# GpSimd's 1024-column subtractions in a one-core transformer layer, issued as two of 512 columns

## The chip, the core and the metric

The kernel runs on one core of a Trainium2 chip. Five engines work side by side, each through its own queue and in order: TensorE (PE in the profile; its weight loads are PEld), VectorE (DVE), ScalarE (ACT), GpSimd (POOL) and SyncE (SP), which here issues nearly all DMAs. They meet through semaphores. The metric is the time on the device in microseconds.

## The reference

One layer of a hybrid transformer: sequence 2048, width 1024, float32. After an RMS norm, a projection to 2576 columns is split over three mixers: differential attention (4 heads with two 64-wide query and key maps each, a bias by distance, causal), a gated linear attention in chunks of 64, and a pooling over windows of 2, 4, 8 and 16 positions. Their outputs are joined, projected and added to the input. Then comes a gated feed-forward part with 2816 hidden columns.

```python
hn = rms_norm(h, attn_norm_g[l])
proj = jnp.einsum('bsd,de->bse', hn, w_in[l])
...
a_out = diff_attention(q, k, v, lam, bias_by_dist)
...
mixed = jnp.concatenate([a_out, b_out, c_out], axis=-1)
h = h + jnp.einsum('bse,ed->bsd', mixed, w_out[l])
hn = rms_norm(h, ffn_norm_g[l])
ff = jax.nn.silu(jnp.einsum('bsd,df->bsf', hn, w_gate[l])) * jnp.einsum('bsd,df->bsf', hn, w_up[l])
h = h + jnp.einsum('bsf,fd->bsd', ff, w_down[l])
```

## The kernel before

**Number format.** Each large product is made of three: an operand x is kept as a high part H, which is x in TensorE's float32r format, and a low part L = x - H in the same format. A product of two such operands is H·H + H·L + L·H. So every weight tile that is loaded has to be split: ScalarE casts it (H), and another engine subtracts (L).

**Stages.** The tokens are handled in four blocks of 512. Phase 1, up to about 620 us, makes the projections of all blocks; its weights are split by ScalarE and VectorE in pieces of 512 columns. Beside it run the gated linear attention and the attention of the first block. Phase 2 makes, block by block, the output projection (L1312 to L1314, eight column tiles), gate and up products (the same lines, or L1384) and the down products (L133, added up by VectorE at L1349), while the attention of blocks 1 to 3 runs beside blocks 0 and 1 until about 1815 us. Blocks 2 and 3 use a scheme with seven instead of eight half-size products (`unit`, L1384), for which sums of weight quarters are formed first (L512 to L515) and sums of activations in `tprep` (L1247 to L1266).

**Weights in phase 2.** `pump` issues the DMA of the next raw weight (L572) when a raw buffer is free, and starts a preparation when one of the ring's weight buffers is free. `wprep` splits a raw weight of 1024 columns: L543 is ScalarE's cast, L544 GpSimd's subtraction, and L548 stores the result for use by later blocks. For blocks 2 and 3 `wpair` fetches the stored split of two quarters and splits the sums of quarters with its helper `hl`: L494 is the cast, L495 the subtraction. A weight buffer holds H in columns 0 to 1023 and L in columns 1024 to 2047. TensorE reads it in row tiles of 128 columns; the low part is the operand of L1314 and of the third product in the down and unit products.

**Attention.** Per unit of 256 queries: scores on TensorE (L133 with the tiles at<-qd and kd, banks 64 to 68), their move out of PSUM by VectorE (L943, with the bias L947), exponentials by ScalarE (L955), the combination of the two maps by VectorE (L963, three operands in SBUF), transposes (L988), and the values product.

**Order.** The Python program spawns generators for these chains and advances them at each `tick`. The order in which an engine gets its instructions is then written by the framework's scheduler (`schedule_with_timeline_sim=True`), which works from its own durations of the instructions. So an instruction of another size can change the order of others, too.

Of the kernel before, what the change touches and what calls it, by code (L numbers as in the profile page):

```python
# [13 lines left out]
ALU = mybir.AluOpType  # L14
# [18 lines left out]
def f(ap):  # L33
    return ap.bitcast(F32)


def r3(ap, a):
    return ap.rearrange("p (a b) -> p a b", a=a)
# [49 lines left out]
def body(nc, tc, V, G, ACT, PE, DMA, A, banks, dram):  # L88
# [354 lines left out]
    def kept(k, i):  # L443

        if (k, i) not in keep:
            keep[k, i] = dram(f"wk{k}{i}", [P, 2048])
        return keep[k, i]
# [35 lines left out]
    def wpair(p):  # L483

        key = pieces[p][0]
        r0, r1 = raws.pop(p)[:, :1024], raws.pop(p + 1)[:, :1024]
        d = W2[key] = {}

        def put(op, w, o):
            d[op] = (r3(w[:, o:o + 512], 4), r3(w[:, 1024 + o:1536 + o], 4), w)  # L490
            uses2[id(w)] = uses2.get(id(w), 0) + 1

        def hl(w, src, o=0, n=1024):
            ACT.copy(w[:, o:o + n], src)  # L494
            G.tensor_tensor(w[:, 1024 + o:1024 + o + n], src, f(w[:, o:o + n]), op=ALU.subtract)  # L495
        k, g = key[0].lower(), key[2]
        w = yield from wring.acq()
        DMA.dma_start(f(w[:, :2048]), kept(k, GS * g))
        put("A11", w, 0)
        put("A12", w, 512)  # L500
        if wst["half"] is None:
            w = yield from wring.acq()
            wst["half"], o = w, 0
            uses2[id(w)] = 1
        else:
            w, o = wst["half"], 512
            wst["half"] = None
            uses2[id(w)] -= 1
        DMA.dma_start(f(r3(w[:, :2048], 2)[:, :, o:o + 512]), r3(kept(k, GS * g + 1), 2)[:, :, 512:1024])
        put("A22", w, o)  # L510
        a11, a12, a21, a22 = r0[:, :512], r0[:, 512:], r1[:, :512], r1[:, 512:]
        V.tensor_tensor(a22, a21, a22, op=ALU.add)  # L512
        V.tensor_tensor(a21, a11, a21, op=ALU.subtract)
        V.tensor_tensor(a11, a22, a11, op=ALU.subtract)
        V.tensor_tensor(a12, a12, a11, op=ALU.subtract)  # L515
        w = yield from wring.acq()
        hl(w, r0)
        put("S2", w, 0)
        put("S4", w, 512)
        w = yield from wring.acq()  # L520
        wst["busy"] = False
        hl(w, r1)
        put("S3", w, 0)
        put("S1", w, 512)
        rawring.rel(wst.pop(("raw", p)), wst.pop(("raw", p + 1)))
# [12 lines left out]
    def wprep(p, w):  # L538
        half, k, src, n = pieces[p]
        raw = raws.pop(p)  # L540
        if n == 0:
            wH, wL = w[:, 0:1024], w[:, 1024:2048]
            ACT.copy(wH, raw[:, :1024])  # L543
            G.tensor_tensor(wL, raw[:, :1024], f(wH), op=ALU.subtract)  # L544
            W2[half] = (r3(wH, KT), r3(wL, KT), w)
            rawring.rel(raw)
            if k is not None:
                DMA.dma_start(k, f(w[:, :2048]))  # L548
            return
        a = KT if n == P else 4  # L550
        wH = r3(w[:, 0:a * n], a)
        wL = r3(w[:, 1088:1088 + a * n], a)
        rv = r3(raw[:, :a * n], a)
        wtile.setdefault((half, k), []).append((wH, wL, w))
        h = a // 2
        ACT.copy(wH[:, :h], rv[:, :h])  # L556
        V.tensor_tensor(wL[:, :h], rv[:, :h], f(wH[:, :h]), op=ALU.subtract)  # L557
        ACT.copy(wH[:, h:], rv[:, h:])
        V.tensor_tensor(wL[:, h:], rv[:, h:], f(wH[:, h:]), op=ALU.subtract)
        rawring.rel(raw)  # L560

    def pump():

        while wst["dma"] < len(pieces) and (rawring.free or pieces[wst["dma"]][3] == -2):
            p = wst["dma"]
            half, k, src, n = pieces[p]
            wst["dma"] += 1
            if n == -2:
                continue
            raw = rawring.free.pop(0)  # L570
            m = KT * P if n in (-1, 0, P) else 4 * n
            DMA.dma_start(raw[:, :m], src.rearrange("p a n -> p (a n)") if len(src.shape) == 3 else src)  # L572
            raws[p] = raw
        if wring.free and wst["prep"] < wst["dma"] and not wst["busy"]:
            p = wst["prep"]
            half, k, src, n = pieces[p]
            if n == -1:
                if p + 1 < wst["dma"]:
                    wst["prep"] += 2
                    wst["busy"] = True  # L580
                    wst["raw", p], wst["raw", p + 1] = raws[p], raws[p + 1]
                    spawn(wpair(p))
            elif n == -2:
                wst["prep"] += 1
                w = wring.free.pop(0)
                DMA.dma_start(f(w[:, :2048]), k)
                W2[half] = (r3(w[:, 0:1024], KT), r3(w[:, 1024:2048], KT), w)
            else:
                wst["prep"] += 1
                spawn(wprep(p, wring.free.pop(0)))  # L590
# [498 lines left out]
    for si, (half, k, b) in enumerate(seq):  # L1089
# [11 lines left out]
        if kind == "e":  # L1101
            bank = force(dense.acq())
            wH, wL, _ = wt[0]
# [12 lines left out]
        else:  # L1116
            n = 272 if i == 2 else 256
# [513 lines left out]
```

## Time and profile before

| | us |
|---|---|
| median of 3 runs | 2679.62 |
| lowest and highest | 2678.34, 2682.49 |
| the profiled execution | 2674.36 |
| its span | 2672.5 |
| TensorE busy | 2537.2 (95%) |
| VectorE busy | 1939.9 (73%) |
| ScalarE busy | 1192.2 (45%) |
| GpSimd busy | 911.0 (34%) |

The span is the time from the first to the last instruction of the profiled execution. Busy shares are means over stages with different limits, so what a change is worth has to be read from the stage that it touches. The chain of waits follows the work that ended last back to what released it.

### The profile page before, as it was taken

What the parts mean: (1) busy time and instruction counts of PE and PEld (TensorE: products, weight loads), DVE (VectorE), ACT (ScalarE), POOL (GpSimd) and SP (SyncE); (2) the same over time, 40 slices, a digit from 0 to 9 for tenths busy, and PEclk for the clock granted to TensorE, in tenths of its full rate; (3) what the DMA queues carried; (4) which work ended last, traced back from release to release, by engine and by line L of the source; (5) the groups of instructions that cost most, each with busy time, mean ns of one, the idle gap of its engine ahead of it and who ended that gap; (6) DMA issues with size and microseconds to landing.
All of it is one profiled execution on the core that took longest, in us unless ns stands there. A gap on an engine that the chain in (4) does not pass through costs nothing.

```text
span 2672.5 us, 38997 instructions
## 1 busy us (share of the span) xinstructions
PE 2537.2 (95%) x14064; PEld 2170.1 (81%) x14064; DVE 1939.9 (73%) x4002; ACT 1192.2 (45%) x2275; POOL 911.0 (34%) x595
## 2 busy tenths in 40 slices
PE   7999889989899999999999999979799999999999
PEld 5887778868778888877788888857688989899998
DVE  7769886689678886885777777775573778766665
ACT  3555545357554454453544444443242333433332
POOL 4235432356644433321322222201423332423331
PEclk8999999989999999999999999989899999999999
DMA  5333644335755645456767667545467665676664
GB/s 166 119 118 103 182 153 151 115 105 189 276 179 159 184 137 183 147 184 214 261 232 245 219 219 248 201 149 182 162 235 274 246 229 191 235 260 225 250 249 167
DMA packets 185518, 517.52 MB, mean 194 GB/s; under 512 B 19067, under 2 KB 63660, under 8 KB 158700
## 3 DMA queue, kind: packets, MB, share of 16 engines
q1 hardware_dynamic: 185036, 515.00, 57.2%
q8 instruction: 111, 1.82, 0.3%
q14 instruction: 83, 0.68, 0.1%
q10 hardware_dynamic: 288, 0.02, 0.0%
HBM read 386.10 MB, written 128.84 MB: 193 GB/s over the span
## 4 chain that ended last, share of the span: by engine, by line
PE 74%; DVE 14%; issue 4%; DMA 3%; ACT 3%; POOL 2%; SPq 0%; DVEq 0%; POOLq 0%; ACTq 0%
PE bk L133 30%; PE bk L1384 14%; PE bk L1313 7%; PE bk L1314 7%; PE bk L1312 7%; PE bk L1108 2%; PE bk L1109 2%; PE bk L1110 2%; PE bk L988 2%; DVE at L963 1%; DVE c L250 1%; DVE c L249 1%; DMA at<-qd 1%; ACT at L955 1%; DVE at L943 1%
## 5 line engine op out<-in xcount | busy, mean ns | idle before, releaser
L133 PE MATMUL bk<-p,c 128*128 128x512 f32 x1136 | 312.2, 399 | 9.9 <-DVE p L217 3.9
L1312 PE MATMUL bk<-c,c 128*128 128x512 f32 x680 | 272.8, 402 | 3.5 <-DMA c<-wko 3.5
L1313 PE MATMUL bk<-c,c 128*128 128x512 f32 x680 | 272.5, 401 | 0.0
L1314 PE MATMUL bk<-c,c 128*128 128x512 f32 x680 | 270.9, 399 | 0.1
L133 PEld LDWEIGHTS bk<-p,c 128*128 128x128 f32 x1136 | 209.3, 190 | 53.5 <-DVE p L217 4.3
L955 ACT ACTIVATE at<-at,at 128x1024 f32<-128x1024 f32 (+4 forms) x192 | 171.6, 895 | 170.2 <-DVE at L952 170.0
L1384 PE MATMUL bk<-c,c 128*128 128x256 f32 x1824 | 239.6, 283 | 0.3 <-ACT c L1390 0.3
L544 POOL TENSOR_TENSOR c<-c,c 128x1024 fp32r<-128x1024 f32 x61 | 151.3, 2483 | 258.8 <-ACT c L543 231.2
L1384 PEld LDWEIGHTS bk<-c,c 128*128 128x128 f32 x1824 | 230.2, 190 | 4.5 <-ACT c L1390 0.7
L1349 DVE TENSOR_TENSOR p<-p,bk 128x512 f32<-128x512 f32 x308 | 204.4, 679 | 34.0 <-PE bk L133 33.3
L943 DVE TENSOR_SCALAR_CACHE_REDUCE at<-bk 128x512 f32<-128x512 f32 (+3 forms) x304 | 154.3, 519 | 86.4 <-PE bk L133 85.0
L1108 PE MATMUL bk<-c,c 128*128 128x512 f32 x448 | 185.1, 415 | 18.6 <-ACT c L556 9.4
L133 PE MATMUL bk<-c,at 128*128 128x512 f32 (+4 forms) x704 | 183.9, 357 | 18.0 <-DMA at<-qd 7.0
L133 PE MATMUL bk<-c,c 128*128 128x256 f32 (+2 forms) x1272 | 184.2, 297 | 6.3 <-DVE p L393 3.1
L1109 PE MATMUL bk<-c,c 128*128 128x512 f32 x448 | 184.5, 412 | 5.2 <-DVE c L250 5.2
L1110 PE MATMUL bk<-c,c 128*128 128x512 f32 x448 | 183.0, 408 | 1.4 <-DVE c L557 1.4
L133 PEld LDWEIGHTS bk<-c,c 128*128 128x128 f32 x1272 | 168.5, 190 | 14.9 <-DVE p L393 4.5
L133 PEld LDWEIGHTS bk<-c,at 128*128 128x128 f32 x704 | 120.5, 193 | 45.5 <-DVE at L943 17.6
L1312 PEld LDWEIGHTS bk<-c,c 128*128 128x128 f32 x680 | 129.0, 190 | 33.2 <-DMA c<-wko 4.2
L1314 PEld LDWEIGHTS bk<-c,c 128*128 128x128 f32 x680 | 128.8, 189 | 29.3 <-POOL c L544 0.5
L1313 PEld LDWEIGHTS bk<-c,c 128*128 128x128 f32 x680 | 129.1, 190 | 28.8 <-DVE c L1184 0.3
L133 PE MATMUL bk<-at,c 128*128 128x256 f32 (+1 forms) x856 | 141.8, 286 | 1.4 <-DVE at L993 0.7
(373 smaller groups left out, 5858.4 us busy)
## 6 DMA issues: line engine op xcount, KB each, us to landing
c<-wkd SPq DMA_DIRECT2D x33, 1024.0 KB, 6.6
c<-w_u SPq DMA_DIRECT2D x56, 512.0 KB, 5.7
c<-w_g SPq DMA_DIRECT2D x55, 512.0 KB, 5.7
wkg<-c SPq DMA_DIRECT2D x21, 1024.0 KB, 4.9
c<-kd SPq DMA_DIRECT2D x72, 256.0 KB, 5.2
c<-vd SPq DMA_DIRECT2D x72, 256.0 KB, 4.4
c<-wko SPq DMA_DIRECT2D x18, 1024.0 KB, 6.0
p<-w_g SPq DMA_DIRECT2D x33, 512.0 KB, 5.5
```

Of the source, the lines that this page charges most:

```text
L133: PE.matmul(out, l, r, start=start and i == 0, stop=stop and i == n - 1)
L544: G.tensor_tensor(wL, raw[:, :1024], f(wH), op=ALU.subtract)
L943: V.tensor_scalar(p[:, c0:c0 + far], pt[:, :far], 1.0, None, op0=ALU.mult, op1=ALU.max, accum_out=mx[:, nx:nx + 1])
L955: ACT.activation(p[:, c0:c1], p[:, c0:c1], AF.Exp, bias=nmx, accum_out=u.z[:, i, m, k:k + 1])
L1108: PE.matmul(bank, wH[:, kt, :], hH[:, kt, :], start=st, stop=False)
L1109: PE.matmul(bank, wH[:, kt, :], hL[:, kt, :], start=False, stop=False)
L1110: PE.matmul(bank, wL[:, kt, :], hH[:, kt, :], start=False, stop=sp)
L1312: PE.matmul(bank, wH[:, kt, :], H[:, kt, :], start=st, stop=False)
L1313: PE.matmul(bank, wH[:, kt, :], L[:, kt, :], start=False, stop=False)
L1314: PE.matmul(bank, wL[:, kt, :], H[:, kt, :], start=False, stop=sp)
L1349: V.tensor_tensor(h2[b][d], h2[b][d], bank, op=ALU.add)
L1384: PE.matmul(out, l[:, k, :], r[:, k, :], start=start and k == 0 and n == 0, stop=k == 3 and n == 2, skip_group_check=True)
```

## The change

Both subtractions of 1024 columns that split weights in phase 2 are issued as two of 512 columns each. The first writes the low part's columns 0 to 511, the second 512 to 1023. The operands, ScalarE's casts and all other lines are as before. A line number behind L495 is higher by one in the changed kernel, one behind L544 by two.

```diff
--- before.py
+++ after.py
@@ -492,7 +492,8 @@
 
         def hl(w, src, o=0, n=1024):
             ACT.copy(w[:, o:o + n], src)
-            G.tensor_tensor(w[:, 1024 + o:1024 + o + n], src, f(w[:, o:o + n]), op=ALU.subtract)
+            for c in range(0, n, 512):
+                G.tensor_tensor(w[:, 1024 + o + c:1536 + o + c], src[:, c:c + 512], f(w[:, o + c:o + c + 512]), op=ALU.subtract)
         k, g = key[0].lower(), key[2]
         w = yield from wring.acq()
         DMA.dma_start(f(w[:, :2048]), kept(k, GS * g))
@@ -541,7 +542,8 @@
         if n == 0:
             wH, wL = w[:, 0:1024], w[:, 1024:2048]
             ACT.copy(wH, raw[:, :1024])
-            G.tensor_tensor(wL, raw[:, :1024], f(wH), op=ALU.subtract)
+            for c in (0, 512):
+                G.tensor_tensor(wL[:, c:c + 512], raw[:, c:c + 512], f(wH[:, c:c + 512]), op=ALU.subtract)
             W2[half] = (r3(wH, KT), r3(wL, KT), w)
             rawring.rel(raw)
             if k is not None:
```

GpSimd's queue at the preparation of block 2's activations (trace 1904 to 1950 us). c, p and pp are weight buffers and raw buffers, tp the activations; first before, then now:

```order
L495 TENSOR_TENSOR pp_14950<-c_102,pp_14950 128x1024
L1242 TENSOR_TENSOR c_72<-tp_15421,c_72 128x1024
L1242 TENSOR_TENSOR c_75<-tp_15422,c_75 128x1024
L495 TENSOR_TENSOR p_6371<-c_103,p_6371 128x1024
L495 TENSOR_TENSOR pp_14950<-p_6372,pp_14950 128x1024
L495 TENSOR_TENSOR pp_14950<-c_102,pp_14950 128x1024
```

```order
L496 TENSOR_TENSOR pp_15066<-c_102,pp_15066 128x512 x2
L1244 TENSOR_TENSOR c_72<-tp_15540,c_72 128x1024
L1244 TENSOR_TENSOR c_75<-tp_15541,c_75 128x1024
L496 TENSOR_TENSOR p_6373<-c_103,p_6373 128x512 x2
L496 TENSOR_TENSOR pp_15066<-p_6374,pp_15066 128x512 x2
L496 TENSOR_TENSOR pp_15066<-c_102,pp_15066 128x512 x2
```

Every row of L495 is now two rows of L496 with half the columns, one directly behind the other, which the listing joins as x2. The order of this stretch is otherwise the same.

TensorE's queue where the third query block's attention runs beside the output projection of block 1 (the matmuls that the trace of before has at about 1230 us). bk are PSUM banks, c_74 is K, at_7945 and at_7964 are Q, c_80 the unit matrix of the transposes, c_72, c_73, c_100 and c_101 are activations and weights of the output projection. Before:

```order
L133 MATMUL bk_66<-at_7962,c_83 128x256
L133 MATMUL bk_64<-c_74,at_7945 128x512 x2
L133 MATMUL bk_66<-c_74,at_7945 128x256 x2
L133 MATMUL bk_66<-c_74,at_7945 128x512 x2
L1312 MATMUL bk_61<-c_72,c_100 128x512
L1313 MATMUL bk_61<-c_73,c_100 128x512
L1314 MATMUL bk_61<-c_72,c_100 128x512
```

The scores that follow there, 24 rows of bk_61 and 18 of bk_62 later:

```order
L1314 MATMUL bk_62<-c_72,c_101 128x512
L133 MATMUL bk_65<-c_74,at_7945 128x384 x2
L988 MATMUL bk_67<-c_80,at_7947 128x128
L988 MATMUL bk_67<-c_80,at_7946 128x128
L988 MATMUL bk_67<-c_80,at_7947 128x128
L133 MATMUL bk_66<-c_74,at_7945 128x512 x2
L988 MATMUL bk_64<-c_80,at_7947 128x128
```

And now:

```order
L1316 MATMUL bk_62<-c_72,c_100 128x512
L1315 MATMUL bk_63<-c_73,c_101 128x512
L1316 MATMUL bk_63<-c_72,c_101 128x512
L990 MATMUL bk_67<-c_80,at_7965 128x128
L133 MATMUL bk_65<-c_74,at_7964 128x384 x2
L133 MATMUL bk_66<-c_74,at_7964 128x512 x2
L990 MATMUL bk_64<-c_80,at_7965 128x128
L133 MATMUL bk_65<-c_74,at_7964 128x512 x2
L133 MATMUL bk_66<-c_74,at_7964 128x384 x2
L1314 MATMUL bk_61<-c_72,c_100 128x512
L1315 MATMUL bk_61<-c_73,c_100 128x512
```

The score products into bk_65 and bk_66 stand ahead of the block of bk_61, which they followed before; the transposes into bk_67 and bk_64 have moved with them. The first instruction that stands elsewhere on any engine is one that the trace of before has at about 620 us. The stretch in which TensorE's queue changes most is 900 to 1310 us, by up to 66 places; later it is mostly groups of twelve matmuls that change places.

## Rows read from the trace of the kernel before

**Rows 1.** The page: busy time, share and instructions of each engine, and the chain of waits by engine.

```profile
PE 2537.2 (95%) x14064; PEld 2170.1 (81%) x14064; DVE 1939.9 (73%) x4002; ACT 1192.2 (45%) x2275; POOL 911.0 (34%) x595
...
PE 74%; DVE 14%; issue 4%; DMA 3%; ACT 3%; POOL 2%; SPq 0%; DVEq 0%; POOLq 0%; ACTq 0%
```

**Rows 2.** Busy time of each engine by stretch: the stretch in us from the span's start, its length, then per engine busy us (instructions), the granted clock, the DMA share and GB/s.

```profile
600.00:800.00 200.00, 186.74 (x964) 155.98 (x964) 154.29 (x299) 120.89 (x249) 112.82 (x78) 0.97 0.65 213
800.00:1100.00 300.00, 298.43 (x1486) 248.59 (x1485) 237.14 (x585) 146.90 (x271) 119.72 (x67) 1.00 0.53 163
1100.00:1300.00 200.00, 187.66 (x926) 154.51 (x925) 142.99 (x341) 88.83 (x176) 52.08 (x33) 0.97 0.61 200
...
1700.00:2000.00 300.00, 257.18 (x1383) 215.97 (x1382) 195.38 (x406) 117.37 (x203) 70.20 (x38) 0.92 0.54 187
2000.00:2673.00 673.00, 661.94 (x4448) 608.69 (x4446) 455.29 (x699) 235.03 (x366) 209.73 (x87) 1.00 0.64 231
```

**Rows 3.** GpSimd's subtraction at L544: duration in ns (least, median, most), first and last start in us; below, who waited for the line, in us and times.

```profile
L544 POOL TENSOR_TENSOR c<-c,c x61: 2372/2409/2921, 620.9 to 1744.3; 128x1024 fp32r<-128x1024 f32 x61
...
  ACT c L543: 10.6, 3
  PEld bk L1314: 3.5, 3
  PE bk L1314: 2.5, 2
```

**Rows 4.** The timeline of GpSimd and of VectorE near 2408 us: start us, us, engine and line.

```profile
2408.28 2.41 POOL L495 TENSOR_TENSOR pp<-p,pp 128x1024 fp32r<-128x1024 f32 x1
...
2408.29 2.95 DVE L1426 TENSOR_TENSOR c<-pp,c 128x512 f32<-128x512 f32 x1
...
2412.98 0.69 DVE L1426 TENSOR_TENSOR pp<-c,pp 128x512 f32<-128x512 f32 x1
```

**Rows 5.** Durations (ns: least, median, most) of three lines of VectorE. L963 and L1339 read their operands in SBUF, L1349 reads a PSUM bank.

```profile
L963 DVE SCALAR_TENSOR_TENSOR at<-at,at,at x160: 336/744/2951, 327.7 to 1812.2; 128x512 f32<-128x512 f32 x112, 128x128 f32<-128x128 f32 x16, 128x256 f32<-128x256 f32 x16, 128x384 f32<-128x384 f32 x16
...
L1339 DVE TENSOR_TENSOR c<-c,c x43: 670/692/2909, 743.0 to 1828.6; 128x512 f32<-128x512 f32 x43
...
L1349 DVE TENSOR_TENSOR p<-p,bk x308: 654/678/690, 761.6 to 2668.4; 128x512 f32<-128x512 f32 x154
```

**Rows 6.** The timeline near 1274 us: two instructions of GpSimd and one of VectorE.

```profile
1273.68 2.41 POOL L544 TENSOR_TENSOR c<-c,c 128x1024 fp32r<-128x1024 f32 x1 [1.57 <-ACT c L543]
1276.05 1.76 POOL L1203 TENSOR_TENSOR p<-p,c 128x512 f32<-128x512 f32 x1
...
1274.85 1.79 DVE L1302 SCALAR_TENSOR_TENSOR c<-p,c,c 128x512 fp32r<-128x512 f32 x1 [0.50 <-ACT c L1301]
```

**Rows 7.** GpSimd's subtractions at L203, which are 512 columns wide: count, busy us and mean ns, then the idle time before them.

```profile
L203 POOL TENSOR_TENSOR p<-p,p 128x512 fp32r<-128x512 f32 x39 | 53.7, 1376 | 87.7 <-DVE p L202 72.9 <-DVE at L924 10.7 <-PE bk L1110 2.1
```

**Rows 8.** Busy time and count of L544 and of L495 on GpSimd over the whole span.

```profile
0.00:2673.00 2673.00, 293.11 (x118) 0.97 0.58 194
...
0.00:2673.00 2673.00, 219.44 (x88) 0.97 0.58 194
```

**Rows 9.** The chain of waits in order of time, the longer pieces: start us, us, what.

```profile
1101.98 2.80 DVE c L1339
...
1131.61 5.97 DVE at L963 x3
...
1149.30 2.29 DVE at L960
...
1151.61 4.02 DVE at L963 x3
...
1192.64 2.44 DVE c L1339
...
1225.28 6.68 DMA c<-wko
...
1280.94 3.42 DVE c L1302 x2
...
1936.58 2.26 DVE c L513
...
1944.12 2.48 DVE pp L1415
...
1983.72 2.16 DVE pp L1426
...
2154.92 2.21 DVE p L1430
2157.13 2.79 DVE c L1426
```

**Rows 10.** The timeline near 957 us: two subtractions of GpSimd and two instructions of VectorE, which stand in one row.

```profile
957.40 2.40 POOL L544 TENSOR_TENSOR c<-c,c 128x1024 fp32r<-128x1024 f32 x1
959.76 2.84 POOL L544 TENSOR_TENSOR p<-p,p 128x1024 fp32r<-128x1024 f32 x1
...
957.44 5.44 DVE L963 SCALAR_TENSOR_TENSOR at<-at,at,at 128x512 f32<-128x512 f32 x2
```

**Rows 11.** TensorE's waits: who waited for whom, us in total, times, the longest us.

```profile
PE bk L133 <- DVE at L943: 6.7, 8, 2.5
...
PE bk L1312 <- DMA c<-wko: 3.5, 2, 3.2
```

## The prediction

> **What bounds the kernel now.** I read the page's first and fourth parts, then the busy time by stretch, then the instructions on GpSimd, VectorE and the chain one by one. The chain of waits is TensorE for 74%, VectorE for 14%, GpSimd for 2% of the span, and GpSimd is busy 911 of 2672.5 us [rows 1]. So the engine that the change touches is not the bound, and its own longer time matters only where somebody waits for it. By stretch [rows 2], TensorE is idle 1.6 us in 800 to 1100 (length less busy time), where there is hardly anything to win. It is idle 13.3 us in 600 to 800, 12.3 in 1100 to 1300, 42.8 in 1700 to 2000 (with the granted clock at 0.92) and 11.1 in 2000 to 2673. Before 617 us no changed instruction runs: the first of the whole-width subtractions at L544 starts at 620.9 [rows 3]. A gain can come from those four stretches alone, some 80 us of idle time.
>
> **What the subtraction does to VectorE.** The trace shows GpSimd's instruction as a lock on a kind of VectorE instruction. At 2408.28 a subtraction of 2.41 us starts, and the L1426 product that starts beside it takes 2.95 us, while the same line takes 0.69 us five microseconds later [rows 4]. 2.95 is 2.41 and the last 0.54. L963 and L1339, which also read two operands in SBUF, take 744 and 692 ns in the median and 2951 and 2909 at most. L1349, which reads one operand in PSUM, never exceeds 690 ns in 308 instructions [rows 5]. So VectorE's instructions with two SBUF inputs wait until the subtraction ends; its evictions from PSUM don't.
>
> The second fact needed is what happens between two GpSimd instructions that follow at once. At 1273.68 a subtraction of 2.41 us runs, followed without a gap by L1203, 512 columns wide, at 1276.05. VectorE's L1302, which started at 1274.85, ends at 1276.64, after the first instruction's end at 1276.09 but long before the second's at 1277.81 [rows 6]. So it is let in at the border between the two, and the second instruction (1.76 us, where another of this width takes 1.38 [rows 7]) pays for it. A border in the middle of the subtraction should therefore let VectorE in there.
>
> **The change, part by part.** It issues 118 + 88 = 206 subtractions, 512.6 us in all [rows 8], 2.49 us each, as 412 of 512 columns. A GpSimd subtraction of this width takes 1.38 us [rows 7]. Per pair that is 2.76 us, 0.27 more; over 206 pairs 56 us more of GpSimd work, which lies beside two thirds of idle time on that engine [rows 1] and costs nothing by itself. The engines' other instructions are the same in number. The border comes 2.49 - 1.38 = 1.11 us before today's end.
>
> Term A, shorter waits of VectorE on the chain. In the stretches where TensorE has idle time, the chain passes through VectorE instructions that are far over their undisturbed time at eleven places [rows 9]. (L963 undisturbed is 0.74, L1339 0.69, the medians in [rows 5]; L1302 and the others of 512 columns are taken as these two.) The row at 1131.61 is three of L963 in 5.97 us instead of 2.22, two waits; 1151.61 and 1280.94 hold one each; with the single ones that makes twelve waits, of 1.5 to 2.1 us. Each is longer than 1.11, so it began before the border, and each would be cut by 1.11 us: 13.3 us if all of it arrives at the end. That is the upper bound. The lower bound is nothing: after the border the second piece is a lock too, and if VectorE's next instruction reads two SBUF operands, it is caught. The rows at 957 us show such a case as it stands today: two subtractions at once, and two L963 between 957.44 and 962.88, each caught by one [rows 10]. Of the twelve I expect this for the three in runs of L963 and for two of the L1430 and L1426 that follow each other at 2154. Seven remain: 7 x 1.11 = 7.8 us. I take **-7.8**.
>
> Term B, the low part is finished later. What waits for the end of a pair, or is caught only in its second half, waits 0.27 us longer. Few instructions wait for L544 directly: ACT's cast three times, TensorE's load three times and its matmul twice [rows 3]; eight waits make 2.2 us. From below it is nothing, since the weights are prepared ahead of use; from above, were all of the 412 pieces stretched by the 0.38 us that letting VectorE in costs [rows 6, 7], it would be 157 us of GpSimd time, still inside its idle time. I take **+2.2**.
>
> Term C, matmuls that can start on half a low part. In the changed program TensorE's third product waits for the first piece, and for the second one only four row tiles later. TensorE's direct waits for L544 are 2.5 us in two matmuls and 3.5 us in three weight loads that overlap them [rows 3]. The first piece comes 1.11 us earlier, twice: **-2.2**; the four row tiles are twelve matmuls, of 298.43 / 1486 = 0.20 us each where TensorE is busy throughout [rows 2], 2.4 us, so the second piece is there in time. Bounds 0 and -2.5.
>
> The new waits (GpSimd's second piece for TensorE's last read of the buffer, SyncE's weight loads for ScalarE's copy as well as GpSimd's piece, VectorE's L513 for the pieces) name work that had to be over before anyway; the instructions queued behind them are the next weight loads and the next sums. I cost them at nothing. If that cover were gone, a weight load would be late, and the largest wait of TensorE for a load of prepared weights today is 3.2 us [rows 11].
>
> Sum: -7.8 + 2.2 - 2.2 = -7.8 us on the profiled execution of 2674.36 us (span 2672.5 and 1.9 around it), 2666.6. The median of the runs shown is 5.3 us above that execution, so I forecast 2671.8, say **2672**.
>
> [...]
>
> **The rivals.**
> *The cut is absorbed.* The second piece catches VectorE's next instruction nearly always, or TensorE is fed by a second path that is as late. For it: two-input instructions stand in rows (L963, L512 to L515), and at 957 us VectorE is held for 4 us [rows 10] in a stretch in which TensorE is nearly never idle [rows 2]. Against it: most evictions read PSUM and pass freely [rows 5]. A is then 0 to -3, and B and C cancel: 2677 to 2680, taken as 2678.
>
> *The new order, slower.* The change also alters the order that the scheduler writes. Where the third query block's attention runs beside the output projection of block 1 (trace 1232 to 1266 us), the score products of one attention unit now stand ahead of a block of 24 output-projection matmuls, which stood ahead of them. TensorE takes its work in order. Where the K, Q or the PSUM bank of those scores isn't free yet, the dense block that filled the time now waits behind them. Today's waits of that kind are on L943, eight, at most 2.5 us [rows 11]. Four new ones of 2.5 us, with A lost, make +10: 2690. It decides from the point where VectorE's eviction of a score bank comes later than TensorE arrives. For it: in 1100 to 1300 TensorE is busy 187.7 of 200 us and runs into waits already [rows 2]. Against it: up to 1232 the chain is a load of the projection's weights [rows 9], for which TensorE waits 3.2 us [rows 11], and the scores now stand in that hole, so the same move may as well win about 5.
>
> *The lock is held through both pieces.* Then every wait of the twelve [rows 9] gets 0.27 us longer instead of 1.11 shorter: 12 x 0.27 = +3.2, and B's 2.2: 2685. [...] Against it stand the rows at 1273 us, where the opening is used [rows 6].
>
> *Everything arrives.* A at its upper bound, C at -2.5 and 5 from the hole at 1232: -21, 2659.
>
> **How the numbers follow.** Forecast 0.45 (its own range 2664 to 2675), absorbed 0.30, new order slower 0.17, lock held 0.03, everything 0.05. What a measurement of this kernel can tell from no change is about 0.2%, 5.4 us: faster is below 2674.3, slower above 2685.0. The forecast gives 0.42 to faster and 0.03 to no change, the last case 0.05 to faster, the absorbed one 0.30 to no change, the order and the lock 0.20 to slower: 0.47, 0.33, 0.20. The range that holds it 8 times in 10 reaches from the last case to the slower order: 2658 to 2690.
>
> **What would show it.** The GpSimd rows at L496 and L546 should come 412 times, at 1.3 to 1.45 us. The longest L963, L1339 and L1426 should fall from 2.9 to about 1.9 us, and VectorE's busy time by some 50 us or more. TensorE's idle time in 1100 to 1300 and in 1900 to 2400 should shrink by about 8 us together, and that in 800 to 1100 stay. If L963 still takes 2.9 us, the lock is held through. If VectorE's busy time falls and the span doesn't, the cut is absorbed. If TensorE's idle time around 1232 to 1266 grows, with L943 or L1053 as the releaser, it was the order. What would make the forecast wrong altogether is a stall of some 10 us in a stretch that has none today.

## The result, and the profile after

The changed kernel takes 2661.36 us (median of 4 runs, 2657.34 to 2664.34), the kernel before 2678.98 on the same chip; the ratio is 0.9938, with a 95% interval of 0.9923 to 0.9953. By the medians it is 17.6 us faster where 7.8 were forecast. The second measurement, on another chip beside two of the experiments, gave 2660.49 (2658.07 to 2661.58) against 2673.92, ratio 0.9944 (0.9932 to 0.9957), 13.4 us faster. It was expected:

> The changed kernel once more, beside the two that follow and the kernel before on the same chip. If the first measurement holds: 0.992 to 0.9955 of the kernel before, some 2658 to 2662 us.

The profiled execution of after took 2664.34 us, the slowest of its four, and that of before 2674.36, less than each of its four (2678.14 to 2682.49); so the two traces differ by 10.0 us only. In the traces below the reader finds those 10 us.

The page's busy times and the chain of waits by engine, which answer to [rows 1]:

```profile
PE 2534.8 (95%) x14064; PEld 2172.2 (82%) x14064; DVE 1885.8 (71%) x4002; ACT 1195.6 (45%) x2275; POOL 973.3 (37%) x801
...
PE 74%; DVE 12%; DMA 4%; issue 3%; ACT 3%; POOL 3%; SPq 0%; POOLq 0%; DVEq 0%; ACTq 0%
```

GpSimd has 206 instructions more and 62 us more work. VectorE has the same 4002 instructions and is busy 54 us less: in those 54 us it was held, not computing. Its share of the chain falls from 14% to 12%.

The lines of the change on GpSimd and of three lines of VectorE after it, as in [rows 3, 5] (count, then ns: least, median, most; first and last start). L965, L1341 and L1351 are L963, L1339 and L1349 of before.

```profile
L546 POOL TENSOR_TENSOR c<-c,c x122: 1260/1298/1752, 622.9 to 1735.3; 128x512 fp32r<-128x512 f32 x122
L965 DVE SCALAR_TENSOR_TENSOR at<-at,at,at x160: 337/746/1811, 328.5 to 1801.8; 128x512 f32<-128x512 f32 x112, 128x128 f32<-128x128 f32 x16, 128x256 f32<-128x256 f32 x16, 128x384 f32<-128x384 f32 x16
L1341 DVE TENSOR_TENSOR c<-c,c x43: 670/692/1694, 747.5 to 1818.2; 128x512 f32<-128x512 f32 x43
L1351 DVE TENSOR_TENSOR p<-p,bk x308: 665/682/693, 766.0 to 2657.9; 128x512 f32<-128x512 f32 x154
```

The medians haven't moved, the longest have: 2951 to 1811 ns and 2909 to 1694. The line that reads PSUM is as before. One more thing is read from these rows in what follows: the last start of L965 (1812.2 before, 1801.8 here) says how early the attention stages end, and the last start of L1351 (2668.4, 2657.9) how early the whole does.

Two places where GpSimd and VectorE meet, to be held against [rows 4, 10]:

```profile
958.81 2.99 POOL L546 TENSOR_TENSOR c<-c,c 128x512 fp32r<-128x512 f32 x2 [1.27 <-ACT c L544]
958.96 3.12 DVE L965 SCALAR_TENSOR_TENSOR at<-at,at,at 128x512 f32<-128x512 f32 x2
...
2398.45 2.99 POOL L496 TENSOR_TENSOR pp<-p,pp 128x512 fp32r<-128x512 f32 x2
2399.02 1.26 DVE L1428 TENSOR_TENSOR c<-pp,c 128x512 f32<-128x512 f32 x1
```

Both pairs of pieces take 2.99 us, where two undisturbed ones take 2 x 1.30. At 2399.02 VectorE's product is done after 1.26 us, although the second piece is queued behind the first. Held to the end of both pieces it would have taken some 2.6 us, an estimate (2398.45 + 2 x 1.30 + the 0.54 of [rows 4] - 2399.02).

TensorE by stretch, as in [rows 2]:

```profile
800.00:1100.00 300.00, 299.93 (x1500) 250.50 (x1499) 232.23 (x597) 150.73 (x274) 131.98 (x108) 1.00 0.54 166
1100.00:1300.00 200.00, 192.56 (x961) 159.04 (x960) 141.32 (x365) 96.02 (x191) 58.45 (x49) 0.97 0.61 202
```

In 1100 to 1300 its idle time falls from 12.3 to 7.4 us. In 1700 to 2000 it is 41.4, after 42.8. But a stretch of fixed times doesn't hold the same work in both kernels: in 1900 to 2400 the idle time falls from 29.0 to 21.2 us, and in 1890 to 2390, where after does that work, it is 27.9. To see where the time came from, the stretches have to be cut at the same instructions. The matmul at L133 that waits for a load from qd into at starts at 764.33 before and 768.05 after, one of block 1's output projection (L1313, now L1315) at 1313.09 and 1302.83. Between them, before and then after:

```profile
764.40:900.00 135.60, 135.60 (x685) 113.74 (x686) 112.18 (x301) 69.34 (x128) 51.96 (x28) 1.00 0.58 175
900.00:1100.00 200.00, 198.43 (x976) 164.64 (x976) 155.48 (x373) 94.73 (x174) 78.04 (x44) 1.00 0.50 156
1100.00:1200.00 100.00, 95.17 (x463) 78.13 (x462) 79.56 (x176) 48.88 (x93) 32.25 (x17) 0.97 0.54 169
1200.00:1313.00 113.00, 104.14 (x508) 84.69 (x507) 73.94 (x203) 50.83 (x106) 26.31 (x20) 0.95 0.67 225
```

```profile
768.10:903.50 135.40, 135.40 (x685) 113.64 (x686) 111.26 (x304) 69.19 (x128) 56.96 (x47) 1.00 0.58 176
903.50:1101.50 198.00, 197.93 (x979) 164.83 (x978) 149.02 (x374) 98.39 (x178) 87.08 (x71) 1.00 0.51 161
1101.50:1196.00 94.50, 92.77 (x462) 76.64 (x461) 72.32 (x173) 47.10 (x90) 34.90 (x28) 1.00 0.52 170
1196.00:1302.70 106.70, 100.99 (x505) 83.37 (x504) 70.78 (x197) 49.14 (x101) 26.25 (x23) 0.95 0.68 231
```

The same work (2632 and 2631 matmuls) takes 548.6 us before and 534.6 after: 14.0 us less, 11.8 of them in the last two rows (213.0 to 201.2). So this stage alone gained more than the kernel. Before 764 us, 3.7 were lost in this execution; the second profile of after reaches the same matmul at 764.45, so that loss needn't be the change's. Behind 1303 us the lead is kept: both last starts above are early by 10.4 and 10.5.

How the 14.0 us divide is the second thing to read there. TensorE's idle time (lengths less busy) falls from 15.3 to 7.5, by 7.8. The waits that went are waits for VectorE: eight lines with 11.8 us before, three with 3.4 after (1.7, 1.2 and 0.5), while for loads TensorE waits 4.7 us in both. The longest before (who waited for whom, us in total, times, the longest us):

```profile
PE bk L133 <- DVE at L943: 4.2, 4, 2.5
PE bk L133 <- DVE p L1195: 2.8, 1, 2.8
PE bk L988 <- DVE at L1053: 1.3, 1, 1.3
```

The second of them, followed back in the timeline of before:

```profile
1280.86 3.50 DVE L1302 SCALAR_TENSOR_TENSOR c<-p,c,c 128x512 fp32r<-128x512 f32 x2
1281.36 2.45 POOL L544 TENSOR_TENSOR c<-c,c 128x1024 fp32r<-128x1024 f32 x1 [3.54 <-ACT c L543]
1284.28 0.68 DVE L1195 TENSOR_TENSOR p<-bk,c 128x512 f32<-128x512 f32 x1
1285.02 0.96 PE L133 MATMUL bk<-p,c 128*128 128x512 f32 x3 [2.82 <-DVE p L1195]
```

GpSimd's subtraction holds the second L1302, L1195 stands behind it in VectorE's queue, and TensorE waits for L1195, which itself takes no longer than elsewhere. In after there is no wait at this place.

TensorE's busy time falls as well, from 533.3 to 527.1, by 6.2, at the same number of matmuls. A part of it lies in stretches with a lower granted clock. Five of before, each behind one or two waits of TensorE, and then the one such stretch of after:

```profile
1156.70:1160.20 3.50, 3.44 (x9) 2.86 (x10) 1.61 (x5) 2.16 (x5) 0.00 (x0) 0.51 0.48 194
1197.80:1201.30 3.50, 3.50 (x15) 3.18 (x14) 3.50 (x7) 2.52 (x5) 0.00 (x0) 0.53 1.07 420
1231.90:1235.40 3.50, 3.40 (x8) 2.73 (x9) 1.57 (x7) 1.77 (x5) 0.00 (x0) 0.52 1.02 290
1286.20:1289.70 3.50, 3.31 (x10) 2.23 (x9) 3.50 (x7) 0.10 (x1) 1.22 (x1) 0.54 0.80 248
1307.00:1310.50 3.50, 3.50 (x10) 2.44 (x8) 2.63 (x11) 2.22 (x5) 0.86 (x1) 0.52 0.97 305
```

```profile
1225.10:1235.30 10.20, 8.41 (x20) 6.22 (x21) 5.34 (x24) 3.57 (x8) 1.13 (x1) 0.51 0.58 225
```

The granted clock is 0.51 to 0.54 there, and 1.00 in 764.40 to 900.00 of before. The timeline of before at the third of them shows the wait ahead of it and the pace (start us, us, what; in brackets the idle time before it and what ended it):

```profile
1232.00 0.80 PE L1312 MATMUL bk<-c,c 128*128 128x512 f32 x1 [3.22 <-DMA c<-wko]
1232.60 0.63 PE L1313 MATMUL bk<-c,c 128*128 128x512 f32 x1
1233.02 0.63 PE L1314 MATMUL bk<-c,c 128*128 128x512 f32 x1
...
1235.44 0.39 PE L1314 MATMUL bk<-c,c 128*128 128x512 f32 x1
1235.67 0.39 PE L1312 MATMUL bk<-c,c 128*128 128x512 f32 x1
```

After 3.22 us of waiting the matmuls start 0.42 us apart, and from 1235.4 on 0.23, where the granted clock is 1.00 (1235.40 to 1238.90). The time lost behind a wait is estimated as the time that TensorE works in such a stretch times (1 - clock): 17.5 x 0.48 = 8.3 us before, 8.4 x 0.49 = 4.1 after. So of the 14.0 us 7.8 are idle time that went and, by this estimate, some 4.2 the stretches with a clock of about 0.5 that had followed the waits; the remaining 2 are busy time that I didn't trace.

### The profile page after: what moved, and what is told of

Same layout as the page of the kernel before. It is cut to its first block, busy times and chain, and to the rows that moved or that the text cites. A ratio compares the mean times of both kernels' runs of the same rounds, so it can differ in the third digit from the quotient of the medians.

```text
span 2662.6 us, 39292 instructions
## 1 busy us (share of the span) xinstructions
PE 2534.8 (95%) x14064; PEld 2172.2 (82%) x14064; DVE 1885.8 (71%) x4002; ACT 1195.6 (45%) x2275; POOL 973.3 (37%) x801
## 4 chain that ended last, share of the span: by engine, by line
PE 74%; DVE 12%; DMA 4%; issue 3%; ACT 3%; POOL 3%; SPq 0%; POOLq 0%; DVEq 0%; ACTq 0%
PE bk L133 30%; PE bk L1386 14%; PE bk L1314 7%; PE bk L1316 7%; PE bk L1315 7%; PE bk L990 2%; PE bk L1110 2%; PE bk L1111 2%; PE bk L1112 2%; DVE c L250 1%; DMA c<-wko 1%; DVE c L249 1%; POOL c L496 1%; DMA at<-qd 1%; DVE c L561 1%
## 5 line engine op out<-in xcount | busy, mean ns | idle before, releaser
L133 PE MATMUL bk<-p,c 128*128 128x512 f32 x1136 | 309.9, 397 | 7.7 <-DVE p L217 5.6
L1315 PE MATMUL bk<-c,c 128*128 128x512 f32 x680 | 272.0, 401 | 0.0
L546 POOL TENSOR_TENSOR c<-c,c 128x512 fp32r<-128x512 f32 x122 | 167.1, 1391 | 254.1 <-ACT c L544 252.1
L133 PEld LDWEIGHTS bk<-p,c 128*128 128x128 f32 x1136 | 206.9, 189 | 50.5 <-DVE p L217 6.4
L1351 DVE TENSOR_TENSOR p<-p,bk 128x512 f32<-128x512 f32 x308 | 206.0, 681 | 43.7 <-PE bk L133 43.1
L133 PE MATMUL bk<-c,at 128*128 128x512 f32 (+4 forms) x704 | 183.9, 358 | 13.7 <-DMA at<-qd 8.4
L133 PE MATMUL bk<-c,c 128*128 128x256 f32 (+2 forms) x1272 | 185.9, 299 | 6.4 <-DVE p L393 4.3
L133 PEld LDWEIGHTS bk<-c,c 128*128 128x128 f32 x1272 | 170.4, 193 | 15.1 <-DVE p L393 5.6
L133 PEld LDWEIGHTS bk<-c,at 128*128 128x128 f32 x704 | 121.1, 194 | 39.8 <-DVE at L949 7.6
L1315 PEld LDWEIGHTS bk<-c,c 128*128 128x128 f32 x680 | 129.1, 190 | 28.4
L133 PE MATMUL bk<-at,c 128*128 128x256 f32 (+1 forms) x856 | 141.7, 285 | 0.7 <-POOL at L1049 0.6
```

The source lines that it names most:

```text
L133: PE.matmul(out, l, r, start=start and i == 0, stop=stop and i == n - 1)
L546: G.tensor_tensor(wL[:, c:c + 512], raw[:, c:c + 512], f(wH[:, c:c + 512]), op=ALU.subtract)
L1315: PE.matmul(bank, wH[:, kt, :], L[:, kt, :], start=False, stop=False)
L1351: V.tensor_tensor(h2[b][d], h2[b][d], bank, op=ALU.add)
```

## The experiments

Each is timed against the kernel before on its own chip (medians 2674.53, 2674.43 and 2673.92). "Attention" is the last start of L963, "end" that of L1349, under whatever number they have there, each against the 1812.2 and 2668.4 of before, in the profiled execution. The first profile of the change has -10.4 and -10.5 there, its second -14.7 and -13.4: two executions of one kernel differ by 3 to 4 us in these columns, and differences of that size between rows show nothing by themselves.

| kernel | us | ratio, interval | attention | end |
|---|---|---|---|---|
| the change, second time | 2660.49 | 0.9944, 0.9932 to 0.9957 | -14.7 | -13.4 |
| wprep in halves alone | 2659.33 | 0.9944, 0.9931 to 0.9956 | -15.6 | -15.0 |
| wpair in halves alone | 2676.46 | 1.0005, 0.9996 to 1.0015 | +0.6 | +0.2 |
| both in four | 2660.26 | 0.9944, 0.9932 to 0.9957 | -19.1 | -14.3 |
| both cut at 960 | 2688.06 | 1.0056, 1.0043 to 1.0068 | +2.7 | +13.3 |
| wprep cut at 960 alone | 2679.37 | 1.0017, 1.0008 to 1.0026 | +0.6 | +3.0 |
| second half first | 2664.40 | 0.9964, 0.9950 to 0.9977 | -7.7 | -10.7 |
| wprep in four alone | 2656.43 | 0.9928, 0.9916 to 0.9940 | -22.9 | -20.7 |
| change, tprep in halves | 2656.31 | 0.9930, 0.9918 to 0.9942 | -14.1 | -17.1 |
| change, tprep on VectorE | 2655.74 | 0.9925, 0.9911 to 0.9938 | -13.8 | -16.9 |
| wprep in four, tprep on VectorE | 2652.32 | 0.9916, 0.9903 to 0.9929 | -19.0 | -22.8 |

**Which of the two places gains.** Only wprep's subtraction (L544) is cut:

```diff
-            G.tensor_tensor(wL, raw[:, :1024], f(wH), op=ALU.subtract)
+            for c, e in ((0, 512), (512, 1024)):
+                G.tensor_tensor(wL[:, c:e], raw[:, c:e], f(wH[:, c:e]), op=ALU.subtract)
```

> Only the subtraction at L544 is split; its order on all engines is that of the changed kernel up to about 1945 us and that of before from there on. Cut waits of VectorE (theory 1): L544 carries the waits of 900 to 1300 us, so most of the gain stays: -10 to -15 us, ratio 0.9945 to 0.9963, with the arrival times of 900 to 1300 us as in the changed kernel. New order (theory 2): the same number, since the order is the same there; this run tells stages apart, not the two theories. If instead the gain comes from blocks 2 and 3: 0 to -4 us.

Then only wpair's (L495), by the same edit there:

> Only the subtraction at L495 is split; the order is that of before up to about 1945 us and that of the changed kernel from there on. Theory 1: five of the twelve chain waits lie here, two of them in a pair that is caught again, and TensorE has 11 us of idle time after 2000 us: -2 to -5 us, ratio 0.998 to 0.9993. Theory 2: the order moves little here, within 2 us of before.

The first holds all of the gain, the second none: within 0.2% of before, where 2 to 5 us were expected of it. The second's last stage, by engine:

```profile
2000.00:2673.00 673.00, 663.24 (x4454) 609.99 (x4452) 434.66 (x703) 236.88 (x370) 233.72 (x165) 1.00 0.65 232
```

VectorE is busy 434.7 us there, after 455.3 in [rows 2], so the relief is there; TensorE is busy 663.2 after 661.9 and gains nothing. Behind 2000 us TensorE has hardly any idle time to give (11.1 us of 673 in [rows 2]); what it waits for near 1900 is shown below.

**Border or order.** The cut moves some 2,600 matmuls in the program. To keep the moved order and take away the border's use, both subtractions are cut at column 960 instead of 512:

```diff
-            for c in (0, 512):
-                G.tensor_tensor(wL[:, c:c + 512], raw[:, c:c + 512], f(wH[:, c:c + 512]), op=ALU.subtract)
+            for c, e in ((0, 960), (960, 1024)):
+                G.tensor_tensor(wL[:, c:e], raw[:, c:e], f(wH[:, c:e]), op=ALU.subtract)
```

> Both subtractions are split at column 960 instead of 512, so that two instructions are issued and the order is close to that of the changed kernel (on TensorE some 1040 matmuls stand elsewhere, against 2590 between before and changed), but the border comes at the very end and VectorE is held about as long as before. Theory 1 (cut waits): no gain, -3 to +4 us, ratio 0.999 to 1.0015; the longest L963 and L1339 stay at 2.7 to 2.9 us. Theory 2 (order): most of the gain stays, -10 to -17 us, ratio 0.9937 to 0.9963. Theory 3 (matmuls that start on the first piece): gone in part, -10 us.

And the same in wprep alone, where the order is within 700 matmuls of that of the kernel with wprep in halves:

> wprep's subtraction cut at column 960, so the border comes 0.15 to 0.2 us before the end; wpair's stays whole. Order up to 1945 us within a few hundred matmuls of the kernel that splits wprep alone in halves, afterwards that kernel's. Theory 1 (the place of the border decides; the order doesn't): 0 at 1300 us, 2674 to 2679 us in all, so 15 us behind the halves at nearly the same order. Rival 2 (the late border itself costs, by pieces of 64 columns and moved releases between 1750 and 1950 us): 2680 to 2684 us. Rival 3 (the order gives the gain): 2659 to 2665 us. It also tells what made the kernel cut at 960 in both places lose 13 us behind 1750 us: if this one stays at the time of before, it was wpair's late border or its order.

VectorE's accumulation in the kernel with wprep in halves, and in the one with wprep cut at 960:

```profile
L964 DVE SCALAR_TENSOR_TENSOR at<-at,at,at x160: 339/746/1821, 327.3 to 1796.6; 128x512 f32<-128x512 f32 x112, 128x128 f32<-128x128 f32 x16, 128x256 f32<-128x256 f32 x16, 128x384 f32<-128x384 f32 x16
```

```profile
L964 DVE SCALAR_TENSOR_TENSOR at<-at,at,at x160: 336/746/2854, 326.2 to 1812.8; 128x512 f32<-128x512 f32 x112, 128x128 f32<-128x128 f32 x16, 128x256 f32<-128x256 f32 x16, 128x384 f32<-128x384 f32 x16
```

As many pieces, nearly the same order, and the longest is 2854 ns again, the attention ends at 1812.8 as before, and the gain is gone. The stage that gained, between the same two matmuls as above, with halves and then cut at 960:

```profile
765.20:1297.90 532.70, 525.72 (x2628) 438.43 (x2628) 404.31 (x1044) 264.39 (x495) 206.45 (x169) 0.99 0.56 181
```

```profile
762.80:1311.80 549.00, 531.45 (x2628) 439.70 (x2629) 416.56 (x1049) 265.40 (x500) 211.91 (x173) 0.99 0.56 178
```

With halves it takes 16 us less, and with the late border as long as before (548.6). TensorE's waits for VectorE in it add up to 3.4 us with halves and to 14.5 with the late border, where the two longest are these:

```profile
PE bk L133 <- DVE p L1196: 3.8, 1, 3.8
PE bk L1313 <- DVE p L1350: 3.3, 1, 3.3
```

So it is the place of the border that gains here, and not the number of instructions; the order gives none of it, as far as two orders that differ by some 700 matmuls can tell. The kernel is even 4.9 us slower than before (interval 2 to 7), just above the 2674 to 2679 us that were expected, so the late border or the order that it brings costs something of its own.

The kernel cut at 960 in both places is 13.5 us slower than before, which lies outside each of the ranges expected. It loses 10 us between 1812 us and the end; cut at 960 in wprep alone it loses 2.4 there, and with wpair in halves nothing. Wpair cut at 960 alone wasn't run, so whether its late border or the order that it brings does this stays open.

**More borders.** Four pieces of 256 in both places, and then in wprep alone:

```diff
-            for c in (0, 512):
-                G.tensor_tensor(wL[:, c:c + 512], raw[:, c:c + 512], f(wH[:, c:c + 512]), op=ALU.subtract)
+            for c, e in ((0, 256), (256, 512), (512, 768), (768, 1024)):
+                G.tensor_tensor(wL[:, c:e], raw[:, c:e], f(wH[:, c:e]), op=ALU.subtract)
```

> Both subtractions are split into four of 256 columns. Theory 1: a wait of VectorE ends at the next of three borders, at most some 0.8 us away plus its own time; the longest L963 falls to about 1.6 us, VectorE's busy time by another 30 to 60 us, and the time by another 2 to 6 us: ratio 0.991 to 0.993 against before. GpSimd's busy time rises to about 1050 us, beside idle time. Theory 2: the order differs from both kernels (4030 matmuls elsewhere against before), so no number follows; anything from -20 to +10 us.

> Four pieces of 256 columns in wprep alone; the subtraction of wpair stays whole. Up to about 1945 us the order is that of the kernel with four pieces in both places, afterwards close to that of before. Theory 1 (four pieces gain 3 to 4 us more than two between 900 and 1310 us, and what was given back behind 1900 us came from wpair's pieces or the order that they bring): 2655 us (2651 to 2658), arrivals 18 us early at 1300 us and still 17 to 19 early at 2300 us. Rival (the late stages wait for work that doesn't move, so an earlier arrival is given back there whatever wpair does): 2660 us (2658 to 2663), 18 early at 1300 and 14 at 2400.

GpSimd and VectorE with four pieces in both:

```profile
L546 POOL TENSOR_TENSOR c<-c,c x244: 723/744/1280, 621.1 to 1728.5; 128x256 fp32r<-128x256 f32 x122
...
L965 DVE SCALAR_TENSOR_TENSOR at<-at,at,at x160: 337/747/1494, 326.5 to 1793.1; 128x512 f32<-128x512 f32 x112, 128x128 f32<-128x128 f32 x16, 128x256 f32<-128x256 f32 x16, 128x384 f32<-128x384 f32 x16
```

The longest of L965 goes 2951, 1811, 1494 ns with one, two and four pieces, and the attention ends 19.1 us early, where the two profiles of the change have 10.4 and 14.7. With four in both places 5 of the 19 are given back by the end, and the time is no better than with two, where 0.991 to 0.993 was expected. With wprep alone in four 20.7 of 22.9 stay, and the time is 2656.4, in the range of 2651 to 2658 that was expected if wpair's pieces or their order did the giving back. The traces agree: in 2250 to 2390 TensorE is idle 7.9 us with four in both places, the longest wait 4.56 us at 2296.64 for ScalarE's cast L494, and 4.5 us with four in wprep alone. But the intervals of the two times overlap, so it is likely and not shown.

**Is the early start on the first piece part of it?** (Term C.) The second half is issued first, in both places:

```diff
-            for c in (0, 512):
-                G.tensor_tensor(wL[:, c:c + 512], raw[:, c:c + 512], f(wH[:, c:c + 512]), op=ALU.subtract)
+            for c, e in ((512, 1024), (0, 512)):
+                G.tensor_tensor(wL[:, c:e], raw[:, c:e], f(wH[:, c:e]), op=ALU.subtract)
```

> Two pieces of 512 columns in both places, as in the changed kernel, but the second half is issued first, so a matmul that reads the first columns finds them last, at the end of both pieces, as before. GpSimd's border stands in the same place for VectorE. Theory 1 (the border lets VectorE in, and that is the whole gain): 2663 us (2657 to 2669), the longest L965 again 1.8 us, VectorE busy about 1886 us. Rival 2 (TensorE's earlier start on the first piece, Term C, carries part of it): the gain falls by that part, 2665 to 2675 us. Rival 3 (the order of the instructions decides, and it moves here more than in any other kernel: about 3400 matmuls): any time from 2650 to 2695 us, with TensorE idle where its first waits are named by a producer that was moved, not by GpSimd.

It gains 10 us where the change gains 13 (second time). The longest of its accumulations is 1870 ns, as with the change. The 3 us between them could be Term C or the order, in which some 3,400 matmuls stand elsewhere than in the changed kernel; the intervals overlap, and this run doesn't tell them apart.

**What the late stage waits for.** Each block's tprep puts two of its subtractions on GpSimd, 1024 wide. The timeline of the changed kernel for GpSimd, VectorE and TensorE, each by itself:

```profile
1903.28 13.21 POOL L1244 TENSOR_TENSOR c<-tp,c 128x1024 fp32r<-128x1024 f32 x2 [5.30 <-ACT c L1243]
```

```profile
1902.83 2.35 DVE L1244 TENSOR_TENSOR c<-tp,c 128x1024 fp32r<-128x1024 f32 x2
1905.10 1.22 DVE L1259 TENSOR_TENSOR tp<-tp,tp 128x1024 f32<-128x1024 f32 x1
1906.24 1.22 DVE L1260 TENSOR_TENSOR tp<-tp 128x1024 f32<-128x1024 f32 x1
1907.37 1.22 DVE L1268 TENSOR_TENSOR tp<-tp,tp 128x1024 f32<-128x1024 f32 x1
1908.51 3.49 DVE L1244 TENSOR_TENSOR c<-tp,c 128x1024 fp32r<-128x1024 f32 x3
```

```profile
1916.54 0.80 PE L1386 MATMUL bk<-c,pp 128*128 128x256 f32 x2 [6.19 <-POOL c L1244]
```

GpSimd needs 13.21 us for two instructions of 2.4. The longest of the line, the first of the two, takes 10.91 us:

```profile
L1244 POOL TENSOR_TENSOR c<-tp,c x4: 2333/2866/10912, 1903.3 to 2294.7; 128x1024 fp32r<-128x1024 f32 x4
```

It ends at 1914.19. VectorE's run from 1902.83 is eight instructions with no pause until 1912.0, and from there GpSimd takes 2.2 us for the first and 2.3 for the second, close to the least of the line, 2333 ns. TensorE waits 6.19 us for the second. First the pair is cut in halves:

```diff
-            e.tensor_tensor(L, src, f(H), op=ALU.subtract)
+            for c in (0, 2) if e is G else ():
+                G.tensor_tensor(L[:, c:c + 2], src[:, c:c + 2], f(H[:, c:c + 2]), op=ALU.subtract)
+            if e is V:
+                V.tensor_tensor(L, src, f(H), op=ALU.subtract)
```

> The changed kernel, and also GpSimd's two subtractions per block in tprep (1024 columns each, about 6.5 us with their waits in the profile, where TensorE waited 6.4 us for them near 1900 us) as two pieces each. Theory 1 (the late stages gained nothing because these unchanged long subtractions hold VectorE and TensorE there): 2 to 6 us faster than the changed kernel, 2657 us (2653 to 2661), and the 6.4 us wait near 1900 us down to 3 to 5. Rival (that wait is set by the chain of ScalarE's casts and VectorE's subtractions ahead of it, not by GpSimd's length): 2662 us, within 2 us of the changed kernel, the wait unchanged.

```profile
1899.70 13.51 POOL L1245 TENSOR_TENSOR c<-tp,c 128x512 fp32r<-128x512 f32 x4 [5.30 <-ACT c L1243]
...
1912.04 1.22 PE L1389 MATMUL bk<-c,pp 128*128 128x256 f32 x4 [6.41 <-POOL c L1245]
```

Four pieces take 13.51 us, and the wait is 6.41: the expected reason is refuted. (That the kernel is 4 us faster than the change was, on another chip, comes from somewhere else, see below; the intervals overlap.) Then the pair is given to VectorE:

```diff
-        hl("T1", T1, G)
+        hl("T1", T1, V)
...
-            hl("B22", b22, G)
+            hl("B22", b22, V)
```

> The changed kernel, with the two subtractions per block that tprep gives to GpSimd put on VectorE. In the changed kernel's profile the one at 1903.28 us takes 10.9 us on GpSimd, and ends 2.1 us after VectorE's run of ten instructions from 1902.83 to 1912.0, with no gap in it, has ended; TensorE waits 6.35 us for the one behind it. Theory (GpSimd is held off by VectorE's unbroken run, the lock in the other direction, so that neither pieces nor length matter, but the engine does): two instructions of 1.2 us more in VectorE's run, its end 2.4 us later, the wait of 6.35 us down to 2 to 4, the time 2 to 5 us below the changed kernel's. Rival (VectorE's longer run delays what stands behind it by as much): within 2 us of the changed kernel's.

(The ten instructions of that text are the eight rows above, its 6.35 us the 6.19.)

```profile
1911.97 1.21 PE L1386 MATMUL bk<-c,p 128*128 128x256 f32 x8 [0.65 <-POOL p L496]
...
1919.99 2.93 PE L1386 MATMUL bk<-c,c 128*128 128x256 f32 x12 [3.74 <-DVE pp L1401]
```

The wait of 6.19 us is gone, as it should be if GpSimd was held by VectorE's unbroken run; what stands there is 0.65, for another line. The time is 4.8 us below the changed kernel's, measured beside it, with intervals that overlap by little. But the wait's end doesn't account for the 4.8 us. Eight us later TensorE now waits 3.74 us for VectorE, and in 1885 to 2000 it is busy 95.3 us, where it was 94.4 in the second profile of the change. Most of the gain lies in 2300 to 2350, where TensorE is busy 49.1 us after 46.0; and the kernel with the pair in halves, whose wait stayed, is busy 48.8 there and as fast (0.9930 and 0.9925 of before). What both gain there stays open.

**The best of both.** Wprep in four, wpair whole, tprep on VectorE:

> Four pieces in wprep alone, wpair whole, and tprep's two subtractions on VectorE: the candidate that should beat both kernels. If the gains add: 0.989 to 0.992 of the kernel before, 2646 to 2653 us, 5 to 12 us below the changed kernel. If the late stages give back what comes early: 0.993 to 0.994, as the changed kernel.

2652.32 us (2651.97 to 2653.23), 0.9916 of the kernel before and 8.2 us below the changed one beside it, in the expected range of 2646 to 2653. Its interval (0.9903 to 0.9929) and the changed kernel's (0.9932 to 0.9957) don't meet. With that of wprep in four alone (0.9916 to 0.9940) it overlaps, so that tprep's move adds to four pieces isn't shown.

## Why the prediction was right, and what it mis-sized

The direction, the lock with its border, and the range (2658 to 2690) were right; the size was half of what came. The 2661.36 us lie outside the forecast's own range (2664 to 2675) and beside the case that had a chance of 0.05, "everything arrives" (2659). That case comes near by luck: its 13.3 us counted five waits behind 1900 us, and its 5 us the hole at 1232, and neither gave anything.

*The lock and its border.* Right. L546 and L496 run at 1.3 us, the longest L963 and L1339 fell to 1.8 and 1.7, VectorE's busy time by 54 us, all as named beforehand. The third rival, the lock held through both pieces, is refuted by the row at 2399.02: the instruction gets in after the first piece (1.26 us), though the second is waiting. To the end of one instruction the lock does hold in the trace, with 2.95 us for VectorE's product beside one instruction of 2.41 [rows 4]; with the cut it is one piece, not the pair, that the product waits for.

*Term A, -7.8, is the mis-sized term.* Of its seven waits of 1.11 us, four lay in 1100 to 1300 (4.4 us) and three behind 1900 (3.3). The stage with the first four gained 14.0 us, 11.8 of them behind 1100; the last three gave nothing: wprep alone gives the first, wpair alone the second. (That TensorE's idle time in the stage fell by 7.8 us, as much as Term A as a whole, is chance.) Three parts of the step failed. It priced a wait of the chain at its idle time, while behind five places of waiting TensorE's granted clock was 0.51 to 0.54 for 3.5 us, which costs, by the estimate above, 1.7 us more apiece; with 8.4 us of such work left of 17.5, that gave 4.2. It counted three of the waits in rows of L963 as caught again by the second piece; the pair at 958.81 shows two L965 done in 3.12 us where [rows 10] had 5.44, so a second instruction is caught, but by a shorter piece. And it took VectorE's late waits in [rows 9] for waits of TensorE that end the stage. In 1880 to 2000 of before TensorE's longest waits are 6.3, 5.6 and 3.6 us for tprep (L1241, L1242), beside 2.2 for L495; with wpair in halves they are 6.6, 4.2 and 3.3, beside 2.4.

*Term B, +2.2.* Not seen by itself. Where only wpair's pairs are longer, the time is 1.9 us above before's, with an interval from 1 us below to 4 us above no change.

*Term C, -2.2.* At most 0.4 us of it is seen. TensorE's two direct waits for the subtraction were 1.71 us at 678.31 and 0.74 at 713.64. The second is 0.31 after; the first is of the same length, with another releaser:

```profile
681.71 0.49 PE L1314 MATMUL bk<-c,p 128*128 128x512 f32 x1 [1.71 <-ACT p L544]
```

The cast ahead of the subtraction, on ScalarE, is what is late next. Issuing the halves in reverse lost 3 us, which may be this term or the order.

*The idle time in 800 to 1100*, which was to stay, fell from 1.6 to 0.1 us. *The new order, slower*, had its place at 1232 to 1266. There the wait for the projection's weights (3.22 us at 1232.00) shrank to 0.61 at 1230.53, and 1.72 us at 1223.62 and 2.33 at 1226.28 came ahead of it; in 1200 to 1250 TensorE is idle 4.5 us before and 4.8 after. With a nearly equal order and no useful border the stage took as long as before (549.0 us), so there the order neither gave nor cost much. What order can cost is seen behind 1812 us at most, in the kernel cut at 960.

## What to carry to other kernels

Where two engines lock each other out by instruction, as GpSimd and VectorE do in these traces (2.95 us for a product of 0.69 beside a whole subtraction, 1.26 beside halves), the length of one instruction of the less loaded engine is a price on the other: cut it, here at some 0.2 us for each cut (0.3 with the longer pieces that let VectorE in: 62 us for 206 cuts), and first where TensorE has idle time behind VectorE. Where the granted clock falls behind a wait of TensorE (here to 0.51 to 0.54 for 3.5 us, five times), price the wait with the slow stretch, not by its idle time. And ask in each stage what is late next: the same cut in wpair freed 20 us of VectorE and moved nothing.

## What the runs showed of the hardware that I had not expected

The lock wasn't always even-handed. GpSimd's two pieces at 2398.45, which follow at once, let VectorE in between them (1.26 us at 2399.02). VectorE's eight instructions from 1902.83, which follow at once too, didn't let GpSimd in: an instruction that takes 2.33 us at the least took 10.91 on GpSimd, to 2.2 us after VectorE's run, and cutting such instructions in two didn't help (13.51 us for the four pieces, 13.21 for the two whole ones). It wasn't so at 958.96: of VectorE's two L965 there the second, 256 columns wide, starts at 960.6 and takes 1.51 us, to 0.3 us after GpSimd's second piece, which came in ahead of it and ends at 961.80. What made the difference wasn't shown. So borders helped VectorE against GpSimd; the other way round they didn't near 1903 us. There GpSimd came in when VectorE paused, and moving the work to VectorE took the wait away, for a shorter one behind it.

TensorE's granted clock was 0.51 to 0.54 in five stretches of 3.5 us in the stage before, behind these waits: 2.46 us at 1156.76, 1.32 and 0.36 at 1196, 3.22 at 1232.00, 2.82 and 0.19 at 1286, 0.45 and 0.79 at 1306. By the estimate above the wait of 3.22 so cost 4.9. Not each wait was followed by it: behind one of 1.46 us at 764.33 the granted clock is 1.00 (764.40 to 767.90). Whether the waits caused it wasn't shown.

GpSimd's subtraction of two fp32 operands took 0.74 us for 256 columns, 1.30 for 512 and 2.41 for 1024 (medians): as an estimate from these three, 0.56 us per 256 columns and some 0.18 us for each instruction.
